# A hybrid transformer step on one core: prompt attention as one list of 64 blocks, sample pages fetched ahead of the sample delta net, other loads of the down projection

## Chip, core and metric

One core of a Trainium2 chip. The metric is the device time of one execution in microseconds; the kernel before took 1775.74 us (median of 3 runs, 1774.68 to 1777.79). One more execution was profiled; it took 1775.13 us, and all times of the trace are taken from it.

## The reference

One decoder layer runs over 1024 prompt tokens and 32 sample tokens (8 sequences of 4), with a width of 1024, and a last norm follows. Everything is fp32.

```python
def stick_breaking(q, k, v, q_pos, k_pos, sb_bias):
    z = einsum(q, k) * d ** -0.5 + sb_bias
    mask = k_pos[None, :] < q_pos[:, None]
    log_1m = where(mask, log_sigmoid(-z), 0.0)
    suffix = cumsum(log_1m, axis=3, reverse=True) - log_1m
    w = where(mask, exp(log_sigmoid(z) + suffix), 0.0)
    return einsum(w, v)
...
h = rmsnorm(x, norm_mix_w)
q_a, k_a, v_a, u, z, a, b, g_a, g_b = split(h @ w_in)
o_a = stick_breaking(...)          # prompt: causal; sample: past pages by page_table, then its own keys
o_b, ssm_new = gdn_branch(short_conv(u), z, a, b, ...)   # gated delta net
y_a = o_a @ w_pa
y_b = o_b @ w_pb
x = x + (sigmoid(g_a) * y_a + sigmoid(g_b) * y_b) @ w_o
x = x + square(relu(rmsnorm(x) @ w_up)) @ w_down
y = rmsnorm(x, norm_final_w)
```

The attention has 8 heads of 64, the delta net 4 heads of 128, the inner width of the MLP is 4096. New keys, values, convolution and delta-net states are outputs as well.

## The kernel before

Activations lie transposed: 8 tiles of 128 features by 1056 tokens, in four token chunks `CX` (256, 256, 256, 288). A dense product is made of three passes, high by high, low by high, high by low part of the split operands (`dense`, lines L137, L138, L139); ScalarE (ACT) rounds the high part and VectorE (DVE) subtracts for the low part when a weight arrives (`load_w`, L123 to L128). PSUM has four pairs of banks: `dtile`, `gtile`, `ttile` and others hand them out.

The stages, by their time in the profile: norm, projections and the prompt's delta net up to about 535 us; the sample delta net (its `drk`, `df` and the like are one-column powers that GpSimd, POOL, computes) to about 600; sample attention over gathered pages (L767 to L874) to 651; prompt attention (`weights`, `attn_head`, `attn_last`, from L881) from 681 on, with the gates' projections (L963 to L976, tiles `pd_g`), the transposes of the residual input (L977 to L988, `xrp`) and the second merge product `y_b` (L1018 to L1053, `pb`, whose operand `obh`, `obl` is read back from DRAM as `ofb`); the first merge product (`pa`) to about 1040; then the output projection, the up projection, and from 1416 the down projection, made of seven products a group of weight blocks (`pw`), with a last part of plain products (`pv`) and the last norm.

Nobody writes the order of the work out. A scheduler takes the program in its order, with the tiles' buffers, `high_priority` sections and `issue_after` marks, and orders each engine's instructions; each engine then runs its own in that order. Nearly all DMAs are issued by SyncE (SP), one after the other in its order: a DMA that waits for a buffer holds up all that stand behind it. The gathers of pages are issued by POOL.

A block of prompt attention is 128 queries of one head against the keys up to them (`weights(hh, i, ...)`, block `i` has 128 x (i + 1) keys). PE makes scores `sc` in two passes (L903, L904); ACT takes their sigmoid into `s` (L905); POOL masks the diagonal (L906) and makes `am` = 1 - s (L909); DVE scans the running product backwards (L913, `pr`) and multiplies (L914); PE transposes `s` by blocks of 128 (`tr`, L111) and ACT copies the result to `wt` (L921); PE multiplies by the values (`po`, L941, L956). Heads 0 to 5 store their output through `oT` in DRAM (`o_d`, read back as `ofa`); heads 6 and 7 run side by side and go straight to `oah3`, `oal3`. `qs`, `kh`, `kl` are loaded for each head and have two buffers.

The gates and residual transposes are in the program behind heads 0 to 5, so that the scheduler takes them when PE would wait; the `pb` products stand behind heads 6 and 7. In the sample attention, keys (`kg`, L819) and values (`vg`, L833) of two pages are gathered for each of 8 sequences, keys transposed to `kts` (L826), in two groups of four sequences.

For the down projection, group 0 loads four weight blocks in quarters (`load_q`, L1368 by its line in the trace, tiles `a11` to `a22`, named `a` in the profile), and for each of seven products four half blocks of the hidden layer (`load_h`, L1360, tile `hc`); `y` takes the residual `x1_d`. The last part loads its weights block by block, both column halves of each.

Of the kernel before, what the change touches and what calls it, by code (L numbers as in the profile page):

```python
# [38 lines left out]
def hybrid_step(ctx, tc, x_prompt, x_sample, cache_k, cache_v, page_table, state_conv, state_ssm,  # L39
# [523 lines left out]
    bk = pool("bk", stack=bctx, side="right")  # L563
    dctx = ExitStack()
# [160 lines left out]
    vk = pool("vk", stack=bctx, side="right")  # L725
# [44 lines left out]
    idx = bk.tile([P, 16], I32, name="idx")  # L770
    nc.scalar.dma_start(idx, page_table.rearrange("s g -> (s g)").unsqueeze(0).to_broadcast([P, 16]))
    rowi = bk.tile([P, 16], I32, name="rowi")
    G.iota(rowi, pattern=[[0, 16]], base=0, channel_multiplier=1)
    V.tensor_scalar(idx, idx, P, None, op0=ALU.mult)
    V.tensor_tensor(idx, idx, rowi, op=ALU.add)
    ckf = cache_k[0].rearrange("n t h d -> (n t) (h d)")
    cvf = cache_v[0].rearrange("n t h d -> (n t) (h d)")

# [32 lines left out]
    vgs = {}  # L811
    for g in range(2):
        psc = ttile(f"dsc{g}")
        kts = []
        for s4 in range(4):
            s = 4 * g + s4
            kg = bk.tile([P, 2, 512], F32, tag="kg", name=f"kg{s}", bufs=2)
            for pg in range(2):
                G.indirect_dma_start(kg[:, pg, :], None, ckf, bass.IndirectOffsetOnAxis(ap=idx[:, 2 * s + pg:2 * s + pg + 1], axis=0))  # L819
            kt = bk.tile([P, 4, 260], F32, tag="kts", name=f"kts{s}", bufs=6)  # L820
            for p2 in range(2):
                pt = (gtile if p2 else dtile)(f"dkt{s}_{p2}")
                for q in range(4):
                    p, pg = 2 * p2 + q // 2, q % 2
                    tr(pt[:, q * P:(q + 1) * P], kg[:, pg, p * P:(p + 1) * P])
                S_.activation(kt[:, 2 * p2:2 * p2 + 2, 0:256], pt.rearrange("p (a f) -> p a f", a=2), AF.Copy)  # L826
            V.tensor_copy(kt[:, :, 256:260], ksT[:, :, 4 * s:4 * s + 4])
            kts.append(kt)
        for s4 in range(4):
            s = 4 * g + s4  # L830
            vgs[s] = vk.tile([P, 2, 512], F32, tag="vg", name=f"vg{s}", bufs=4)
            for pg in range(2):
                G.indirect_dma_start(vgs[s][:, pg, :], None, cvf, bass.IndirectOffsetOnAxis(ap=idx[:, 2 * s + pg:2 * s + pg + 1], axis=0))  # L833
# [5 lines left out]
        ds_ = bk.tile([P, n], F32, tag="ds", name=f"ds{g}", bufs=2)  # L839
# [40 lines left out]
    ak = pool("ak", 2, stack=actx, side="right")  # L880

# [14 lines left out]
    def weights(hh, i, qs, kh, kl):  # L896
        n = P * (i + 1)
        qsl = slice(i * P, n)
        s = ak.tile([P, NP], F32, tag="s", name=f"s{hh}_{i}", bufs=6)
        for k0 in range(0, n, 512):  # L900
# [3 lines left out]
            PE.matmul(pt[:, :kn_], lhsT=qs[:, qsl], rhs=kl[:, k0:k0 + kn_], start=False, stop=True)  # L904
# [9 lines left out]
        V.tensor_tensor(s[:, :n - 1], s[:, :n - 1], pr[:, 1:n], op=ALU.mult)  # L914
        wt = ak.tile([P, NP], F32, tag="wt", name=f"wt{hh}_{i}", bufs=2)
# [7 lines left out]

    def load_v(p):
# [4 lines left out]
    def attn_head(hh, vn):  # L929
        p, a = hh // 2, hh % 2  # L930
        rs = slice(64 * a, 64 * a + 64)
        ops = attn_load(hh)
        oT = ak.tile([P, NC // 2, P], F32, tag="oT", name=f"oT{hh}")
        for m in range(NC // 2):
            wts = [weights(hh, 2 * m + r, *ops) for r in range(2)]
            po = gtile(f"po{hh}_{m}")
            for b in range(2 * m + 2):
                for r in range(2):
                    if b > 2 * m + r:
                        continue  # L940
                    PE.matmul(po[64 * r:64 * r + 64, 0:P], lhsT=vn[:, b, rs], rhs=wts[r][:, b * P:(b + 1) * P],  # L941
                              start=(b == 0), stop=(b == 2 * m + r))
            S_.activation(oT[:, m, :], po[:, 0:P], AF.Copy)
        for r in range(2):
            SY.dma_start(o_d[p, rs, 0:NP].rearrange("d (m r c) -> d r m c", r=2, c=P)[:, r], oT[64 * r:64 * r + 64])

    def attn_last(oh, ol):
        vn = load_v(3)
        ops = [attn_load(6), attn_load(7)]
        for i in range(NC):  # L950
            wts = [weights(6 + a, i, *ops[a]) for a in range(2)]
            po = gtile(f"po6_{i}")
            for b in range(i + 1):
                for a in range(2):
                    rs = slice(64 * a, 64 * a + 64)
                    PE.matmul(po[rs, 0:P], lhsT=vn[:, b, rs], rhs=wts[a][:, b * P:(b + 1) * P], start=(b == 0), stop=(b == i))  # L956
            cs_ = slice(i * P, (i + 1) * P)
            S_.activation(oh[:, cs_], po[:, 0:P], AF.Copy)
            V.tensor_tensor(ol[:, cs_], po[:, 0:P], oh[:, cs_].bitcast(F32), op=ALU.subtract)

    for p in range(3):
        vn = load_v(p)
        attn_head(2 * p, vn)  # L963
        attn_head(2 * p + 1, vn)


    for j in range(KT):
        for b, gd in ((0, gA_d), (1, gB_d)):
            gt = fk.tile([P, T], F32, tag="ft", name=f"gt{b}_{j}", bufs=NFT)

            def ev(c, o, n, pt, gt=gt):
                with tc.high_priority():
                    S_.activation(gt[:, o:o + n], pt[:, :n], AF.Sigmoid)

            proj([(3592 + b * D + j * P, f"g{b}_{j}", ev)], f=True)
            SY.dma_start(gd[j], gt)  # L976
    for t in range(9):  # L977
# [24 lines left out]
    attn_last(oah3, oal3)  # L1002
# [18 lines left out]
    for c in (3, 0, 1):  # L1021
        ob_tiles(c)
    with tc.high_priority():
        S_.activation(obh[0], ofb0, AF.Copy)
        V.tensor_tensor(obl[0], ofb0, obh[0].bitcast(F32), op=ALU.subtract)
    for c, (o, n) in enumerate(CX):
        if c == 0:
            continue
        for k in range(4):
            st = obp.tile([P, 288], F32, tag="of", name=f"ofb{c}{k}", bufs=3)  # L1030
            if c == 1 and k == 0:
                ob_tiles(2)
            mark = SY.dma_start(st[:, :n], o_d[4 + k, :, o:o + n])
            with tc.high_priority():
                S_.activation(obh[c][:, k], st[:, :n], AF.Copy)
                V.tensor_tensor(obl[c][:, k], st[:, :n], obh[c][:, k].bitcast(F32), op=ALU.subtract)
        if c == 1:
            with tc.issue_after(mark.ins):
                for j in range(2):
                    SY.dma_start(tbs[j], gB_d[j])  # L1040
    for jp in range(4):
        wb = load_w(wpbv[:, :, jp * 256:(jp + 1) * 256], f"pb{jp}")
        for jj in range(2):
            j = 2 * jp + jj
            tb = tbs[j]
            if jp:
                with tc.issue_after(mark.ins), tc.issue_after(wq[0].ins):
                    SY.dma_start(tb, gB_d[j])
            for c, (o, n) in enumerate(CX):
                pt = dtile(f"pb{j}_{c}", f=True)  # L1050
                dense4(pt, wb, jj, [obh[c][:, k] for k in range(4)], [obl[c][:, k] for k in range(4)], n)
                with tc.high_priority():
                    V.tensor_tensor(tb[:, o:o + n], pt[:, :n], tb[:, o:o + n], op=ALU.mult)  # L1053
    ofa = []
    for k in range(2):
        st = (zp if k == 0 else z2p).tile([P, T], F32, tag="zz", name=f"ofa{k}")
# [27 lines left out]
    for jp in range(4):  # L1084
        wa = load_w(wpav[:, :, jp * 256:(jp + 1) * 256], f"pa{jp}")
        for jj in range(2):
# [5 lines left out]
            for c, (o, n) in enumerate(CH):  # L1092
# [260 lines left out]

    def split2(tl):
# [181 lines left out]
```

## Time and profile before

| | |
|---|---|
| runs | 1775.74 us median, 1774.68 to 1777.79 |
| profiled execution | 1775.13 us, span 1773.2 us, granted clock 0.988 |
| sample attention, 600 to 660 us | PE busy 50.1 of 60 |
| prompt attention with gates, 680 to 760 | PE busy 78.1 of 80, DVE 48.1 |
| prompt attention with residual transposes, 760 to 840 | PE busy 72.4 of 80, DVE 61.6 |
| heads 6 and 7 with `pb`, 840 to 900 | PE busy 55.3 of 60, DVE 49.4 |
| up to the down projection, 1040 to 1380 | PE busy 336.7 of 340 |
| into the down projection, 1380 to 1420 | PE busy 34.8 of 40 |
| down projection, 1420 to 1690 | PE busy 269.9 of 270 |
| from 1763 to the end | PE busy 4.5 of 10 |

The busy time of PE is modelled: a matmul that stands alone shows 0.28 us, though in a row the next one starts 0.12 us later. So a stage with many lone matmuls shows more busy time than work.

### The profile page before, as it was taken

The page shows a single profiled execution, that of the slowest core. Times are in us where ns is not written, and L with a number is a line of the kernel's source. Part 1 is how long each engine was busy: PE and PEld are TensorE (multiplying, and loading weights), DVE is VectorE, ACT ScalarE, POOL GpSimd, SP SyncE. Part 2 cuts the span into 40 slices and gives each one's busy share as a digit, 9 for nine tenths or more (in the row PEclk, how much of TensorE's full clock was granted, in tenths as well). Part 3 has the DMA queues.
Part 4 walks back from the last instruction along what each step waited for, and adds up shares of the span by engine and source line. Part 5 has one row for each costly group of instructions (what it writes and reads, how often), then busy time and mean ns, then how long its engine had stood idle before and what let it go on. Part 6 is the DMA issues. An engine that isn't in the chain of part 4 may idle for free.

```text
span 1773.2 us, 34494 instructions
## 1 busy us (share of the span) xinstructions
PE 1710.3 (96%) x13884; PEld 1646.6 (93%) x13884; DVE 1156.5 (65%) x2312; ACT 785.3 (44%) x1563; POOL 205.0 (12%) x239
## 2 busy tenths in 40 slices
PE   7999999999999889999899999999999899999998
PEld 6999999999999668977789999999999899999998
DVE  6665777767234213677947577877777778788853
ACT  5553444343323223566523445555445555434454
POOL 1120111110001322356500000000000000000000
PEclk9999999999999889999999999999999999999999
DMA  5142232234335546578323544645444684432421
GB/s 175 43 119 77 56 115 78 90 104 145 113 106 153 181 133 160 143 186 231 125 96 121 163 145 134 171 140 149 148 141 134 216 303 146 156 112 94 135 84 75
DMA packets 233579, 239.22 MB, mean 135 GB/s; under 512 B 22754, under 2 KB 192067, under 8 KB 233420
## 3 DMA queue, kind: packets, MB, share of 16 engines
q1 hardware_dynamic: 229110, 228.40, 42.2%
q0 software_dynamic: 2560, 8.39, 1.5%
q8 instruction: 109, 1.79, 0.4%
q10 hardware_dynamic: 1750, 0.23, 0.1%
q14 instruction: 50, 0.41, 0.1%
HBM read 163.21 MB, written 73.77 MB: 134 GB/s over the span
## 4 chain that ended last, share of the span: by engine, by line
PE 70%; issue 12%; POOL 6%; DVE 6%; DMA 4%; ACT 1%; SPq 0%; POOLq 0%; DVEq 0%; ACTq 0%; another core or an unknown queue 0%
PE pu L139 6%; PE pu L137 6%; PE pu L138 6%; PE pw L138 5%; PE pw L137 5%; PE pw L139 5%; POOL am L909 3%; POOL s L906 2%; PE px L138 1%; PE px L139 1%; PE pv L137 1%; PE px L137 1%; PE pv L139 1%; PE pv L138 1%; PE pd_g L137 1%
## 5 line engine op out<-in xcount | busy, mean ns | idle before, releaser
L137 PE MATMUL pu<-Xh,uh 128*128 128x264 f32 x812 | 229.8, 283 | 1.0 <-ACT uh L1135 1.0
L139 PE MATMUL pu<-Xh,ul 128*128 128x264 f32 x812 | 230.1, 284 | 0.0
L138 PE MATMUL pu<-Xl,uh 128*128 128x264 f32 x812 | 229.7, 283 | 0.0
L137 PE MATMUL pw<-hc,w 128*128 128x264 f32 x728 | 206.7, 286 | 5.2 <-ACT w L1382 5.2
L138 PE MATMUL pw<-hc,w 128*128 128x264 f32 x728 | 207.0, 287 | 0.0
L139 PE MATMUL pw<-hc,w 128*128 128x264 f32 x728 | 201.7, 284 | 0.0
L137 PEld LDWEIGHTS pu<-Xh,uh 128*128 128x128 f32 x812 | 153.1, 189 | 1.2 <-ACT uh L1135 1.2
L138 PEld LDWEIGHTS pu<-Xl,uh 128*128 128x128 f32 x812 | 152.7, 188 | 0.0
L138 PE MATMUL pd_g<-xl,wh_g 128*128 128x256 f32 (+1 forms) x512 | 149.0, 291 | 3.2 <-issue 3.2
L139 PEld LDWEIGHTS pu<-Xh,ul 128*128 128x128 f32 x812 | 152.0, 188 | 0.0
L137 PE MATMUL pd_g<-xh,wh_g 128*128 128x256 f32 (+1 forms) x512 | 149.8, 293 | 1.4 <-issue 0.8
L139 PE MATMUL pd_g<-xh,wl_g 128*128 128x256 f32 (+1 forms) x512 | 149.9, 293 | 0.3 <-issue 0.3
L137 PEld LDWEIGHTS pw<-hc,w 128*128 128x128 f32 x728 | 137.8, 189 | 5.4 <-ACT w L1382 5.4
L138 PEld LDWEIGHTS pw<-hc,w 128*128 128x128 f32 x728 | 137.5, 189 | 0.0
L139 PEld LDWEIGHTS pw<-hc,w 128*128 128x128 f32 x728 | 135.4, 188 | 0.0
L913 DVE TENSOR_TENSOR_SCAN pr<-am 128x127 f32<-128x127 f32 (+7 forms) x64 | 89.8, 1403 | 43.0 <-POOL am L909 42.9
L138 PEld LDWEIGHTS pd_g<-xl,wh_g 128*128 128x128 f32 x512 | 97.6, 191 | 7.4 <-issue 7.1
L137 PEld LDWEIGHTS pd_g<-xh,wh_g 128*128 128x128 f32 x512 | 97.6, 191 | 6.2 <-issue 4.8
L139 PEld LDWEIGHTS pd_g<-xh,wl_g 128*128 128x128 f32 x512 | 97.5, 190 | 4.8 <-issue 4.6
L1382 ACT ACTIVATE w<-a 128x512 fp32r<-128x512 f32 x78 | 43.4, 623 | 94.3 <-PE pw L139 88.5
L114 POOL TENSOR_TENSOR fr<-fr,powc 128x3 f32<-128x3 f32 x4 | 3.4, 858 | 679.0 <-DVE fr L1493 643.2
L139 PE MATMUL px<-mh,wl_wo 128*128 128x264 f32 x256 | 72.7, 287 | 1.3 <-DVE wl_wo L1136 1.2
(581 smaller groups left out, 5198.7 us busy)
## 6 DMA issues: line engine op xcount, KB each, us to landing
hc_d<-t SPq DMA_DIRECT2D x26, 924.0 KB
hc<-hc_d SPq DMA_DIRECT2D x91, 264.0 KB
a<-in_w_down_dram SPq DMA_DIRECT2D x52, 256.0 KB
ws_g<-in_w_in_dram SPq DMA_DIRECT2D x16, 512.0 KB
ws_wo<-in_w_o_dram SPq DMA_DIRECT2D x32, 256.0 KB
ua<-in_w_up_dram SPq DMA_DIRECT2D x16, 512.0 KB
ub<-in_w_up_dram SPq DMA_DIRECT2D x16, 512.0 KB
gA_d<-gt SPq DMA_DIRECT2D x8, 528.0 KB
```

What stands on the lines that cost most here:

```text
L114: G.tensor_tensor(out, in_, powc[: out.shape[0], which:which + 1].to_broadcast([out.shape[0], n]), op=ALU.pow)
L137: PE.matmul(pt[:, :n], lhsT=wh[k], rhs=xh[k], start=(k == 0), stop=False)
L138: PE.matmul(pt[:, :n], lhsT=wh[k], rhs=xl[k], start=False, stop=False)
L139: PE.matmul(pt[:, :n], lhsT=wl[k], rhs=xh[k], start=False, stop=(k == nk - 1))
L906: G.affine_select(s[:, qsl], s[:, qsl], pattern=[[-1, P]], compare_op=ALU.is_gt, fill=0.0, base=0, channel_multiplier=1)
L909: G.tensor_scalar(am[:, :n], s[:, :n], -1.0, 1.0, op0=ALU.mult, op1=ALU.add)
L913: V.tensor_tensor_scan(pr[:, n - 1:0:-1], am_r, am_r, 1.0, op0=ALU.mult, op1=ALU.bypass)
L1382: S_.activation(tl[:, 0], src, AF.Copy)
```

## The change

**Sample pages.** Index, keys and values of sequences 0 to 3 move ahead of the sample delta net; the values' pool `vk` goes, `kts` has 4 buffers in place of 6. The keys and values of 4 to 7 stay in group 1 of the sample attention.

**Attention.** `weights` is cut in two: `scores` (up to the product on DVE) and `transposed` (transposes and copy). The 64 blocks become one list: heads 0 to 5, then 6 and 7 in turns with `i` descending. `pipeline` walks through it: scores of block x + 4, then transposes of block x (marked to stand behind those scores), then fillers, then the value products. Eleven of the 16 gates come before the list, five gates and nine residual steps fill blocks 0 to 33, and the 32 `pb` steps fill blocks 34 to 63. `s` keeps 6 buffers (LAG + 2). The residual step has one `xr` and one `xs` buffer, and stores in two halves. The operand of `pb` is read in four pieces instead of thirteen.

**Behind it.** The first merge product takes its token chunks in reverse.

**Down projection.** In group 0, the first four `hc` and the first weight quarter go to POOL's queue, the other loads are chained in the order of need, and `y` is loaded in halves between. In the last part, the first column halves of all weights and the hidden halves come first; the last square of the norm has a tile of its own, which PE adds in.

```diff
+    for s in range(4):
+        keys(s)
+        values(s)
     dctx = ExitStack()
     dk = pool("dk", stack=dctx, side="right")
...
-    vk = pool("vk", stack=bctx, side="right")
...
     for g in range(2):
         psc = ttile(f"dsc{g}")
+        if g:
+            for s in range(4, 8):
+                keys(s)
+        kts = [kts_[4 * g + s4] for s4 in range(4)]
...
+    blks = [(hh, i) for hh in range(6) for i in range(NC)] + [(6 + a, i) for i in range(NC - 1, -1, -1) for a in range(2)]
+    SPLIT = 34
...
+    def stage_b(x, fill):
+
+        ahead = state[min(x + LAG, NB - 1)][1]
+        with tc.issue_after(ahead.ins):
+            wts[blks[x]] = transposed(blks[x], state[x][0])
+        for f in fill:
+            f()
+        values_of(blks[x])
+
+    def pipeline(x0, x1, fill):
+
+        done = 0
+        for x in range(x0, x1):
+            stage_a(x + LAG)
+            upto = len(fill) * (x + 1 - x0) // (x1 - x0)
+            stage_b(x, fill[done:upto])
+            done = upto
...
+    def residual_step(t):
         n = P if t < 8 else NS
-        xn = fk.tile([P, D], F32, tag="ft", name=f"xr{t}", bufs=NFT)
+        xn = ak.tile([P, D], F32, tag="xr", name=f"xr{t}", bufs=1)
...
+    for j, b in gjobs[:11]:
+        for f in gate_steps(j, b):
+            f()
+    for x in range(LAG):
+        stage_a(x)
...
+    pipeline(0, SPLIT, fills)
...
-    attn_last(oah3, oal3)
...
+    steps = [lambda j=j, c=c, f=(x == 0): pb_step(j, c, f) for j in range(KT) for x, c in enumerate(range(4))]
+    pipeline(SPLIT, NB - 2, steps[:-6])
+    pipeline(NB - 2, NB, steps[-6:])
...
-            for c, (o, n) in enumerate(CH):
+            for c, (o, n) in reversed(list(enumerate(CH))):
...
+                        if i == 0:
+                            load_part(q, f, nm, G)
+                        else:
+                            queued(lambda: load_part(q, f, nm))
+            for n, f in enumerate(fs):
+                ld = lambda: load_h(hc_d[f - NPL, i], f"hc{f}_{i}", G if gi == 0 and i == 0 else SY)
+                hs[n] = queued(ld) if gi == 0 and i else ld()
...
+    for c in range(2):
+        for i, f in enumerate(fl):
             cs_ = slice(c * HD2, (c + 1) * HD2)
...
+                PE.matmul(pf[:n, i:i + 1], lhsT=sa[:, t * P:t * P + n], rhs=ones[:, 0:1], start=True, stop=False)
+                PE.matmul(pf[:n, i:i + 1], lhsT=sl[:, t * P:t * P + n], rhs=ones[:, 0:1], start=False, stop=True)
```

The rows below are the engines' instructions in the order of the built programs; a name ends with a number that tells buffers of one name apart.

POOL, between the masks of the delta net and the first mask of the prompt attention, before: `kg` and `vg` are gathers of keys and values, x2 the two pages of a sequence; `drk` and `df` belong to the sample delta net.

```order
L576 AFFINE_SELECT ms_4286<-ms_4286 128x256
L819 DMA kg_6126<-in_cache_k_dram,idx 128x512 x2
L819 DMA kg_6143<-in_cache_k_dram,idx 128x512 x2
L114 TENSOR_TENSOR drk<-drk_4352,powc 128x1
L114 TENSOR_TENSOR df<-df,powc 128x1
L819 DMA kg_6160<-in_cache_k_dram,idx 128x512 x2
L819 DMA kg_6177<-in_cache_k_dram,idx 128x512 x2
L833 DMA vg_6194<-in_cache_v_dram,idx 128x512 x2
L833 DMA vg_6197<-in_cache_v_dram,idx 128x512 x2
L833 DMA vg_6200<-in_cache_v_dram,idx 128x512 x2
L833 DMA vg_6203<-in_cache_v_dram,idx 128x512 x2
```

The same place now:

```order
L624 AFFINE_SELECT ms_4368<-ms_4368 128x256
L594 DMA kg_4283<-in_cache_k_dram,idx 128x512 x2
L607 DMA vg_4299<-in_cache_v_dram,idx 128x512 x2
L594 DMA kg_4302<-in_cache_k_dram,idx 128x512 x2
L607 DMA vg_4318<-in_cache_v_dram,idx 128x512 x2
L607 DMA vg_4337<-in_cache_v_dram,idx 128x512 x2
L607 DMA vg_4356<-in_cache_v_dram,idx 128x512 x2
L114 TENSOR_TENSOR drk<-drk_4434,powc 128x1
L594 DMA kg_4321<-in_cache_k_dram,idx 128x512 x2
L594 DMA kg_4340<-in_cache_k_dram,idx 128x512 x2
L594 DMA kg_6261<-in_cache_k_dram,idx 128x512 x2
```

Twelve gathers stand ahead of `drk` instead of four; five key pairs follow, then `df`, then one key pair and four value pairs, ten gathers in a row.

PE, at the end of head 3 and the start of head 4, before: `sc_2_0` is the score of block 2 from key 0 on, `wt_7_4` transposes of block 7 from key block 4 on, `po_3` the value products of blocks 6 and 7.

```order
L111 MATMUL wt_6_0_7265<-ident,s_6_7249 128x128 x2
L111 MATMUL wt_6_4_7271<-ident,s_6_7249 128x128 x3
L903 MATMUL sc_2_0_7372<-kh_7326,qs_7325 128x384
L904 MATMUL sc_2_0_7372<-kl_7327,qs_7325 128x384
L903 MATMUL sc_3_0_7389<-kh_7326,qs_7325 128x512
L904 MATMUL sc_3_0_7389<-kl_7327,qs_7325 128x512
L941 MATMUL po_3_7304<-wt_6_7264,vn_6865 64x128
L111 MATMUL wt_7_0_7292<-ident,s_7_7276 128x128 x4
L111 MATMUL wt_7_4_7298<-ident,s_7_7276 128x128 x4
L903 MATMUL sc_4_0_7416<-kh_7326,qs_7325 128x512
L904 MATMUL sc_4_0_7416<-kl_7327,qs_7325 128x512
```

PE now, in the middle of head 3, with gate products `pd_g`:

```order
L137 MATMUL pd_g_7_3_9070<-xh_167,wh_g_7_8780 128x288
L138 MATMUL pd_g_7_3_9070<-xl_168,wh_g_7_8780 128x288
L932 MATMUL sc_0_0_9050<-kh_9041,qs_9040 128x128
L933 MATMUL sc_0_0_9050<-kl_9042,qs_9040 128x128
L111 MATMUL wt_4_0_9061<-ident,s_4_8871 128x128 x4
L139 MATMUL pd_g_7_3_9070<-xh_167,wl_g_7_8781 128x288
L137 MATMUL pd_g_7_3_9070<-xh_167,wh_g_7_8780 128x288
L138 MATMUL pd_g_7_3_9070<-xl_168,wh_g_7_8780 128x288
L980 MATMUL po_1_9029<-wt_3_9022,vn_8266 64x128
L980 MATMUL po_1_9029<-wt_2_8983,vn_8266 64x128
```

In heads 3 to 5 PE had only `sc`, `wt`, `po` and `xrp`; now gate products stand between them up to block 33, and `pb` from there on.

SP, where `pb` begins, now (with what each waits for; a wait for DMAHW is for an earlier DMA in the same one of eight lanes): `ofb` is an operand of `pb`, `tb` a gate read back, `kh`, `kl` and `qs` are the operands of head 6 (9848 to 9850) and head 7 (9896 to 9898).

```order
L919 DMA kh_9849<-kh_d 64x1024 [waits DMAHW6_49]
L1119 DMA ofb_9417<-o_d 128x4x256 [waits DMAHW7_49]
L920 DMA kl_9850<-kl_d 64x1024 [waits DMAHW0_49]
L1148 DMA ofa_10723<-o_d 128x1056 [waits DMAHW1_49,DVE_49]
L1119 DMA ofb_9423<-o_d 128x4x288 [waits DMAHW2_49,DVE_49]
L1135 DMA tb_9394<-gB_d 128x1056 [waits DMAHW3_49]
L1135 DMA tb_9395<-gB_d 128x1056 [waits DMAHW4_49]
L1135 DMA tb_9396<-gB_d 128x1056 [waits DMAHW5_49]
L1135 DMA tb_9397<-gB_d 128x1056 [waits DMAHW6_49]
L985 DMA o_d<-oT_9367 64x4x128 [waits DMAHW7_49,Activation_49]
L1148 DMA ofa_10725<-o_d 128x1056 [waits DMAHW2_49,DMAHW1_49,DVE_49]
L919 DMA kh_9897<-kh_d 64x1024 [waits PE_49]
```

The loads of head 7 stand behind the gates read back and the store of head 4 (`oT_9367`); before, the gates read back stood behind them.

SP at the start of the down projection, before, with the first weight quarters `a` behind the twelfth `hc` load:

```order
L1360 DMA hc_2_17064<-hc_d 128x528
L1308 DMA hc_d<-t_16571 128x7x264
L1360 DMA hc_2_17068<-hc_d 128x528
L1360 DMA hc_2_17072<-hc_d 128x528
L1368 DMA a_3_16720<-in_w_down_dram 128x512
L1368 DMA a_3_16722<-in_w_down_dram 128x512
```

POOL now holds the first eight of these loads:

```order
L1453 DMA hc_0_16722<-hc_d 128x528
L1453 DMA hc_0_16726<-hc_d 128x528
L1453 DMA hc_0_16730<-hc_d 128x528
L1453 DMA hc_0_16734<-hc_d 128x528
L1461 DMA a_3_16702<-in_w_down_dram 128x512
L1461 DMA a_4_16707<-in_w_down_dram 128x512
L1461 DMA a_5_16712<-in_w_down_dram 128x512
L1461 DMA a_6_16717<-in_w_down_dram 128x512
```

They no longer stand behind the twelve `hc` loads of SP, and the second quarters follow on SP.

More of the change, by code (lines that the diff above doesn't have):

```diff
@@ L810, in hybrid_step @@
     osT = bk.tile([P, 4, NS], F32, name="osT")
-    vgs = {}
     for g in range(2):
         psc = ttile(f"dsc{g}")
-        kts = []
+        if g:
+            for s in range(4, 8):
+                keys(s)
+        kts = [kts_[4 * g + s4] for s4 in range(4)]
         for s4 in range(4):
             s = 4 * g + s4
[L817 to L833, printed above, removed]
+            V.tensor_copy(kts[s4][:, :, 256:260], ksT[:, :, 4 * s:4 * s + 4])
+            if g:
+                values(s)
         for p in range(4):
@@ L947, in attn_last @@
[L947 to L976, printed above, removed]
@@ L1019, in ob_tiles @@
         obl[c] = obp.tile([P, 4, CX[c][1]], F32R, name=f"obl{c}")
-    for c in (3, 0, 1):
+    for c in range(len(CX)):
         ob_tiles(c)
-    with tc.high_priority():
-        S_.activation(obh[0], ofb0, AF.Copy)
-        V.tensor_tensor(obl[0], ofb0, obh[0].bitcast(F32), op=ALU.subtract)
     for c, (o, n) in enumerate(CX):
         if c == 0:
[L1028 to L1053, printed above, removed]
+            st = ofb0
+        else:
+            if c == 1:
+                st = z2p.tile([P, 4, 288], F32, tag="zz", name="ofb1")[:, :, 0:256]
+            elif c == 2:
+                st = obp.tile([P, 4, 256], F32, name="ofb2")
+            else:
+                st = z2p.tile([P, 4, 288], F32, tag="zz", name="ofb3")
+            mark = SY.dma_start(st, o_d[4:8, :, o:o + n].rearrange("k p c -> p k c"))
@@ new lines, in hybrid_step, with pb_step @@
+        with tc.high_priority():
+            S_.activation(obh[c], st, AF.Copy)
+            V.tensor_tensor(obl[c], st, obh[c].bitcast(F32), op=ALU.subtract)
+        if c == 2:
+            for j in range(2):
+                SY.dma_start(tbs[j], gB_d[j])
+    wbs = {}
+    def pb_step(j, c, first):
+        jp, jj = j // 2, j % 2
+        if jp not in wbs:
+            wbs[jp] = load_w(wpbv[:, :, jp * 256:(jp + 1) * 256], f"pb{jp}")
+        tb = tbs[j]
+        if jp and first:
+            with tc.issue_after(mark.ins), tc.issue_after(wq[0].ins):
+                SY.dma_start(tb, gB_d[j])
+        o, n = CX[c]
+        pt = dtile(f"pb{j}_{c}", f=True)
+        dense4(pt, wbs[jp], jj, [obh[c][:, k] for k in range(4)], [obl[c][:, k] for k in range(4)], n)
+        with tc.high_priority():
+            V.tensor_tensor(tb[:, o:o + n], pt[:, :n], tb[:, o:o + n], op=ALU.mult)
```

233 lines of the change are left out of this document (168 added, 65 removed).

## Prediction

> **What bounds the kernel now.** I read the engine shares first, then the windows by stage, the timeline for the pace of one matmul, and the waits of the stages that fall short. Columns of the windows: the stretch, its length, busy us (instructions) of PE, PEld, DVE, ACT, POOL, the granted clock, the DMA share, GB/s.
>
> ```profile
> PE 1710.3 (96%) x13884; PEld 1646.6 (93%) x13884; DVE 1156.5 (65%) x2312; ACT 785.3 (44%) x1563; POOL 205.0 (12%) x239
> ```
>
> ```profile
> 680.00:760.00 80.00, 78.14 (x633) 70.42 (x632) 48.07 (x47) 39.10 (x90) 27.23 (x44) 1.00 0.54 139
> 760.00:840.00 80.00, 72.37 (x564) 58.49 (x563) 61.61 (x58) 52.76 (x118) 49.19 (x54) 0.96 0.86 227
> 840.00:900.00 60.00, 55.28 (x444) 46.25 (x444) 49.42 (x66) 30.63 (x70) 26.02 (x30) 1.00 0.33 112
> 900.00:940.00 40.00, 37.31 (x283) 35.39 (x280) 19.94 (x35) 9.43 (x13) 0.00 (x0) 1.00 0.37 120
> 1420.00:1690.00 270.00, 269.93 (x2214) 269.71 (x2213) 216.76 (x406) 121.13 (x219) 0.00 (x0) 1.00 0.47 160
> ```
>
> TensorE bounds the kernel: the change can only win what it loses in a few places. In the long dense stage it loses nothing (2214 matmuls in 270 us, 0.122 each). The busy column hides losses, since a matmul that trickles still shows 0.28 us, so I count work by pace, start to start, from a stretch without idle:
>
> ```profile
> 713.94 0.34 PE L903 MATMUL sc<-kh,qs 128*128 128x384 f32 x1
> 714.11 1.03 PE L111 MATMUL wt<-ident,s 128*128 128x128 f32 x8
> 714.90 0.42 PE L904 MATMUL sc<-kl,qs 128*128 128x384 f32 x1
> 715.16 0.39 PE L903 MATMUL sc<-kh,qs 128*128 128x512 f32 x1
> 715.39 0.40 PE L904 MATMUL sc<-kl,qs 128*128 128x512 f32 x1
> 715.63 0.29 PE L137 MATMUL pd_g<-xh,wh_g 128*128 128x288 f32 x1
> ...
> 716.42 0.28 PE L137 MATMUL pd_g<-xh,wh_g 128*128 128x256 f32 x1
> ...
> 717.82 1.96 PE L941 MATMUL po<-wt,vn 128*64 128x128 f32 x28
> 719.71 0.55 PE L111 MATMUL wt<-ident,s 128*128 128x128 f32 x3
> ```
>
> A transpose costs 0.79/8 = 0.099 us, a 512-wide score 0.235 (0.45 ns a column), a 288-wide product 0.79/6 = 0.132, a value product 1.89/28 = 0.0675. Attention has 64 blocks: 8 x 2 x 4608 score columns (33 us), 288 transposes (28.5), 576 value products (39), 101 us, or 1.6 a block. Beside it stand in 680 to 940 us the fillers:
>
> ```profile
> L139 PE MATMUL pd_g<-xh,wl_g 128*128 128x256 f32 (+1 forms) x115 | 33.3, 290 | 0.0
> L139 PE MATMUL pb<-obh,wl_pb 128*128 128x256 f32 (+1 forms) x128 | 37.1, 290 | 0.0
> L111 PE MATMUL xrp<-ident,xr 128*128 128x128 f32 (+1 forms) x72 | 9.2, 268 | 0.8 <-DMA xr<-in_x_prompt_dram 0.8
> L913 DVE TENSOR_TENSOR_SCAN pr<-am 128x127 f32<-128x127 f32 (+7 forms) x64 | 89.8, 1403 | 43.0 <-POOL am L909 42.9
> L914 DVE TENSOR_TENSOR s<-s,pr 128x127 f32<-128x127 f32 (+7 forms) x64 | 53.0, 832 | 4.0
> ```
>
> (columns: line, engine, operation, tiles, shapes and count | busy us, mean ns of one | idle before and its releaser). Gates 3 x 115 x 0.122 = 42 us, merge products 3 x 128 x 0.122 = 47, residual transposes 7, and the first 62 products of the next stage 10 (0.17 each, as the 384-wide score): 207 to 209 us of work in 260, so **about 51 us are lost here**. The stretch that mixes gates in best, 700 to 760, holds (rows of one pass; scores and gates have two and three):
>
> ```profile
> L139 PE MATMUL pd_g<-xh,wl_g 128*128 128x256 f32 x61 | 17.5, 286 | 0.0
> L941 PE MATMUL po<-wt,vn 128*64 128x128 f32 x144 | 13.1, 280 | 0.0
> L111 PE MATMUL wt<-ident,s 128*128 128x128 f32 x77 | 11.2, 279 | 0.4 <-DVE s L914 0.4
> L903 PE MATMUL sc<-kh,qs 128*128 128x512 f32 x12 | 5.4, 448 | 0.0
> L913 DVE TENSOR_TENSOR_SCAN pr<-am 128x767 f32<-128x767 f32 (+7 forms) x17 | 23.7, 1392 | 18.9 <-POOL am L909 18.9
> ```
>
> 21.5 us of gates 256 wide, 6.3 of gates 288 wide, 9.7 of value products, 7.6 of transposes, 9 of scores (25 matmuls 512 wide and 26 narrower): 54 of 60, 5.8 lost over 17 blocks. By the same count 24 us are lost from 760 to 840, 12 from 840 to 900, 4.5 from 680 to 700, 4.3 from 900 to 940. The reason is VectorE: scan and product take 142.8/64 = 2.23 us a block against PE's 1.6. Heads 3 to 5 have 7 us of residual transposes beside them, and PE waits.
>
> **Attention.** The list of 64 blocks keeps the work and spreads the fillers. Gates left for the attention: five (480 products, 58 us) over 34 blocks with the residual steps (7): 54 + 65 = 119 us PE against 34 x 2.23 = 76 DVE. The merge products (47) go over the last 30, longer blocks: 47 + 47 = 94 us and some 5 of the next stage, against 68 us of scans and products on VectorE and what these rows hold:
>
> ```profile
> L1053 DVE TENSOR_TENSOR tb<-pb,tb 128x256 f32<-128x256 f32 (+1 forms) x32 | 13.4, 426 | 18.2 <-PE pb L139 17.1 <-DMA tb<-gB_d 1.0
> L128 DVE TENSOR_TENSOR wl_pb<-ws_pb,wh_pb 128x1024 fp32r<-128x1024 f32 x4 | 4.9, 1223 | 0.5 <-ACT wh_pb L127 0.5
> ```
>
> 13.4 and 4.9, and 9 for the splits of the attention's outputs (my estimate, some eight tiles of that size): 95. PE leads in both halves, if closely in the second. The lag of four blocks is 4 x 3.5 = 14 us (60 us over 17 blocks), and of a block's chain (score copy, mask, `am`, scan, product) the two costliest steps are 2.2. So what stays is what 700 to 760 shows, 5.8 us over the 17 blocks scanned there, 0.34 a block: 22 us; a start as before (680 to 700: 4.5 lost, 3 beyond that rate); the end as before, 4; and I put 4 for the point where the merge products begin (below). 51 - 33 = **18 us gained**; ends 8 (DVE bounds the last 30 blocks with the losses of 840 to 900, 0.2 of the time) and 32 (change-overs cost half, nothing else stays). A residual step now has one `xr` and one `xs` buffer, so each waits for the store of the one before; 2 to 4 blocks lie between, 7 us or more, and I cost it at nothing. The reversed order in the next stage, too: it takes first what the descending blocks finish first.
>
> **Sample pages.** Each gather holds POOL 0.95 + 0.30 us. Two runs of twelve stand here, and PE, DVE and ACT crawl from some 7.6 us after a run's first gather to 6 us after its last:
>
> ```profile
> 599.37 1.02 POOL L819 DMA_INDIRECT kg<-in_cache_k_dram,idx  x1 [16.30 <-PE dkt L111]
> ...
> 613.23 0.95 POOL L833 DMA_INDIRECT vg<-in_cache_v_dram,idx  x1 [0.30 <-issue]
> ...
> 630.65 0.94 POOL L819 DMA_INDIRECT kg<-in_cache_k_dram,idx  x1 [9.00 <-PE dkt L111]
> ...
> 644.44 0.95 POOL L833 DMA_INDIRECT vg<-in_cache_v_dram,idx  x1 [0.30 <-issue]
> ```
>
> ```profile
> 535.00:555.00 20.00, 19.48 (x163) 19.21 (x161) 11.79 (x43) 12.38 (x23) 4.66 (x5) 1.00 0.82 246
> 607.00:621.00 14.00, 9.20 (x39) 6.54 (x38) 0.00 (x0) 2.94 (x6) 8.80 (x10) 0.63 0.74 238
> 638.00:652.00 14.00, 8.94 (x41) 5.75 (x43) 1.18 (x3) 2.45 (x5) 5.70 (x6) 0.63 0.48 144
> ```
>
> 39 and 41 matmuls at 0.12 are 4.8 us of each 14: 9.2 lost twice, 18.4. The four gathers near 540 cost nothing. The change does not break the runs: POOL's order has twelve in a row at about 540 (keys and values of four sequences), then pairs, then ten (the last keys and all later values). The first moves its 9.2 us to about 548; ten crawl for 12.5 + 6 - 7.6 = 11 us instead of 13.4, 7.5 lost. Gain 1.7, say **2**. Ends: 18 if the crawl came from something else at 600, and -7: `drk`, a power on POOL of the sample delta net, now stands behind twelve gathers, some 9 us late, and its chain waits while PE has gate products; with no cover that is all lost.
>
> **Down projection, start.** PE stands still between 1411 and 1416 for the first weight quarter, behind 12 loads of `hc` in SP's queue:
>
> ```profile
> 1407.69 4.67 SPq L1368 DMA_DIRECT2D a<-in_w_down_dram  x5
> ```
>
> ```profile
> 1408.00:1412.00 4.00, 3.05 (x26) 2.85 (x24) 4.00 (x10) 1.95 (x4) 0.00 (x0) 1.00 1.07 370
> 1412.00:1416.00 4.00, 0.00 (x0) 0.00 (x0) 2.37 (x5) 3.17 (x6) 0.00 (x0) 1.00 1.05 371
> 1416.00:1420.00 4.00, 3.73 (x18) 3.73 (x19) 4.00 (x9) 0.85 (x2) 0.00 (x0) 0.57 1.00 373
> 1690.00:1695.00 5.00, 3.71 (x29) 3.28 (x27) 4.61 (x9) 3.41 (x6) 0.00 (x0) 1.00 0.49 185
> ```
>
> 44 matmuls in 12 us are 5.3 us of work: 6.7 lost, clock at 0.57 included. Now POOL issues the four `hc` and four first quarters, 2.1 MB, 5.6 us at 370 GB/s, released by a product that the order puts some 95 matmuls, 11.6 us, before the up projection's end. I take **4**; ends 0, and 6.7. A loss is bounded by an eight-long run that crawls as above for 8 us: -4. The Trainium skill, DMA: Bandwidth & Descriptors, section Issuing engines are not separate DMA queues, speaks against this part: all issuers share the 16 engines, and a second one "will only save the time on the sequencer". By it this term would be 0 and the sum 1754; the share of 1.0 agrees that the engines are full, but the row of SP shows an order, not a rate, that kept the quarter back.
>
> **Last part.** 29 products in 5 us from 1690 are 3.5: 1.5 lost to weights that come late; the first column halves now come first: **1** (0 to 1.5). The tail's squares skip one VectorE addition and add nine one-column products: nothing, +-0.5.
>
> **Sum.** 18 + 2 + 4 + 1 = 25 us. The profiled execution took 1775.1 (span 1773.2), 0.6 below the median of the runs, 1775.7: 1775.1 - 25 = **1750**.
>
> **Rivals.** (1) SP's queue where the merge products begin; slower. Between head 4's last score and head 7's first, 29 us of PE work (26 by pace, 9 blocks of change-over), SP must issue in order head 6 (1.5 MB), two pieces of the merge operand and `ofa` (1.6), four gates read back (2.1), head 4's store, `ofa` and head 7 (2.3): 7.8 MB. The stage 760 to 840 moved 227 GB/s at a share of 0.86, 264 when full: 29.5 us, just enough, hence my 4 us. All PE work stands in order behind those operands. At 160 GB/s it takes 49 us, a stall of 20: 1766. From 141 GB/s down (55 us) the 26 us cancel every gain: at 120, 65 us, about **1782**. Against it: no busy stage here was so slow. (2) VectorE bounds the last 30 blocks, as 840 to 900 (49.4 of 60 busy, 12 lost): gain 8, and no gain at the pages: **1765**. For it: 95 against 99. (3) The crawl goes with the place and the change-overs shrink: 32 + 12 + 5: **1730**. (4) Page run and `drk` cost 7, the eight-run 4, the switch 15 more: gains cancel, about **1775**. That the change isn't made is excluded by the order of the built program.
>
> **Chances.** Forecast (1738 to 1762) 0.58; rival 3 0.10; rival 2 with half of rival 1 (1762 to 1772) 0.14; rival 4 0.07; rival 1 slower 0.11. A measurement of this kernel tells some 0.2% (3.5 us) from no change: faster 0.82, within 0.07, slower 0.11. The range reaches from the unknown costs' good ends to rival 2's far side: 1732 to 1771.
>
> **What would show it.** Right: 760 to 840 at over 640 matmuls in 80 us, no scan-bound stretch; a crawl with clock near 0.6 at about 550 and one of ten gathers later; no empty window at the start of down. Wrong: PE waiting for `kh`, `obl` or `tb` around the first merge products (rival 1), `wt` waiting for `s` on DVE in the last heads (rival 2), `drk`'s readers idle with PE idle too.

## The result, and the profile after

The changed kernel took 1753.82 us (median of 4 runs, 1751.82 to 1755.30) against 1776.53 before; the ratio is 0.9859, with a 95% interval of 0.9842 to 0.9876. Forecast were 1750, and 25 us gained; measured are 22.7. The profiled execution took 1754.63 us, 20.5 less than the profiled one of before. So the total came out close to the forecast. Its terms did not, as the experiments show.

The windows of the changed kernel, with the same columns as before, at the stages that the prediction spoke of:

```profile
541.00:555.00 14.00, 13.39 (x113) 13.11 (x112) 7.38 (x22) 11.23 (x21) 11.26 (x10) 1.00 0.88 269
555.00:569.00 14.00, 9.69 (x86) 6.79 (x86) 1.96 (x5) 1.39 (x3) 6.52 (x8) 0.66 0.60 194
618.00:632.00 14.00, 13.73 (x129) 9.94 (x127) 2.74 (x6) 2.81 (x5) 8.48 (x8) 1.00 0.63 196
660.00:680.00 20.00, 17.51 (x119) 15.49 (x120) 12.01 (x13) 10.21 (x23) 10.22 (x16) 0.91 0.77 206
680.00:740.00 60.00, 60.00 (x502) 53.32 (x499) 40.66 (x37) 35.59 (x79) 25.89 (x34) 1.00 0.71 187
740.00:800.00 60.00, 59.65 (x481) 52.16 (x481) 32.93 (x35) 31.93 (x71) 19.27 (x30) 1.00 0.60 155
800.00:820.00 20.00, 16.95 (x138) 13.32 (x139) 18.62 (x19) 12.58 (x27) 14.37 (x14) 1.00 1.05 322
820.00:900.00 80.00, 80.00 (x673) 71.47 (x671) 58.96 (x74) 34.94 (x71) 25.69 (x37) 1.00 0.29 85
740.00:820.00 80.00, 76.60 (x618) 65.49 (x618) 51.55 (x53) 44.51 (x96) 33.64 (x44) 1.00 0.71 197
760.00:840.00 80.00, 76.80 (x593) 64.99 (x592) 59.00 (x57) 43.26 (x91) 37.97 (x41) 1.00 0.67 186
```

PE is full from 680 to 800 and from 820 to 900, with 8.0 to 8.4 matmuls a us, where before the stretches from 760 to 900 held 7.1 to 7.4. Two holes are left in the attention, at its start (660 to 680) and where the merge products begin (800 to 820). The second lies in the stretch for which I had named a sign, over 640 matmuls from 760 to 840: there are 593 (564 before), so this sign did not come. One crawl is left beside the gathers, at 555 to 569 with the clock at 0.66; beside the later gathers (618 to 632) there is none. What PE waited for from 640 to 675, and then from 795 to 822 (the wait, us in total, times, the longest):

```profile
PE xrp L111 <- DMA xr<-in_x_prompt_dram: 2.3, 1, 2.3
PE sc L933 <- DMA kl<-kl_d: 0.7, 1, 0.7
...
PE pb L138 <- DVE obl L1122: 2.1, 2, 1.7
PE pb L137 <- ACT wt L954: 0.5, 1, 0.5
PE pb L137 <- ACT obh L1121: 0.4, 1, 0.4
```

Where the down projection starts, the windows (and one of the last part), then ACT's timeline (start, us, engine, line, operation, count, idle before it):

```profile
1388.00:1392.00 4.00, 2.19 (x19) 1.99 (x17) 0.96 (x3) 2.56 (x5) 0.00 (x0) 1.00 1.04 364
1392.00:1396.00 4.00, 3.41 (x16) 3.41 (x17) 3.88 (x8) 3.49 (x8) 0.00 (x0) 0.57 0.83 309
...
1422.00:1430.00 8.00, 6.99 (x55) 6.56 (x55) 8.00 (x14) 7.36 (x15) 0.00 (x0) 1.00 0.53 183
...
1669.00:1674.00 5.00, 4.60 (x36) 4.19 (x35) 4.69 (x9) 4.95 (x11) 0.00 (x0) 1.00 0.49 184
```

```profile
1381.98 2.24 ACT L1448 ACTIVATE hc<-hc 128x528 fp32r<-128x528 f32 x4
1389.24 0.65 ACT L1390 ACTIVATE t<-t 128x528 f32<-128x528 f32 x1 [5.03 <-DVE t L1386]
...
1391.37 0.64 ACT L1391 ACTIVATE t<-t 128x528 f32<-128x528 f32 x1
1391.92 1.13 ACT L1475 ACTIVATE w<-a 128x512 fp32r<-128x512 f32 x2
```

The empty window is gone, and the loads come in time: ACT split the four `hc` by 1384. But the first weight quarter's split stands in ACT's order behind the last squares of the up projection, and so behind PE's last up product. The wait for a load has become a wait for ACT's order, 2.8 us from the last `pu` to the first `pw` where it was 5.6; and in 1422 to 1430, with DVE full, 55 products stand where 66 would fit (1.3 us).

### The profile page after: what moved, and what is told of

Read it like the earlier page. It is cut to its first block, busy times and chain, and to the rows that moved or that the text cites. A ratio compares the mean times of both kernels' runs of the same rounds, so it can differ in the third digit from the quotient of the medians.

```text
span 1752.9 us, 34523 instructions
## 1 busy us (share of the span) xinstructions
PE 1704.8 (97%) x13902; PEld 1645.2 (94%) x13902; DVE 1148.9 (66%) x2299; ACT 783.2 (45%) x1554; POOL 206.6 (12%) x247
## 3 DMA queue, kind: packets, MB, share of 16 engines
q10 hardware_dynamic: 1750, 0.23, 0.1%
## 4 chain that ended last, share of the span: by engine, by line
PE 74%; issue 8%; DMA 6%; DVE 6%; POOL 3%; ACT 1%; SPq 1%; POOLq 0%; DVEq 0%; ACTq 0%
PE pu L139 6%; PE pu L137 6%; PE pu L138 6%; PE pw L139 4%; PE pw L138 4%; PE pw L137 4%; PE pd_g L137 2%; POOL am L938 2%; PE pd_g L139 2%; PE pd_g L138 2%; POOL s L935 1%; PE px L138 1%; PE px L137 1%; PE px L139 1%; PE pv L137 1%
## 5 line engine op out<-in xcount | busy, mean ns | idle before, releaser
L138 PE MATMUL px<-ml,wh_wo 128*128 128x264 f32 x256 | 72.6, 285 | 0.0
```

Of the source, the lines that this page charges most:

```text
L138: PE.matmul(pt[:, :n], lhsT=wh[k], rhs=xl[k], start=False, stop=False)
```

## Experiments

The kernels of the table ran on three chips, here A, B and C, each beside the kernel before, which took 1778.9, 1763.6 and 1780.8 us there; so sizes are read as ratios to it, or between kernels of one chip.

| kernel | chip | us | ratio to before (95%) |
|---|---|---|---|
| pages as before (`gath_back`) | A | 1772.96 | 0.9964 (0.9950 to 0.9977) |
| attention as before (`attn_back`) | A | 1763.14 | 0.9899 (0.9875 to 0.9923) |
| down's loads as before (`down_back`) | A | 1756.01 | 0.9863 (0.9840 to 0.9886) |
| last part as before (`last_back`) | A | 1753.04 | 0.9853 (0.9828 to 0.9878) |
| gathers broken up (`paced`) | B | 1745.70 | 0.9908 (0.9883 to 0.9933) |
| all gates ahead (`gates16`) | B | 1765.13 | 1.0013 (0.9999 to 1.0028) |
| pages as before, 14 gates ahead (`gath_back_g14`) | B | 1752.84 | 0.9946 (0.9924 to 0.9968) |
| lag of one block (`lag1`) | B | 1752.52 | 0.9944 (0.9926 to 0.9962) |
| changed kernel (`after_again`) | C | 1754.22 | 0.9850 (0.9827 to 0.9872) |
| gathers broken up (`paced_again`) | C | 1756.69 | 0.9867 (0.9846 to 0.9889) |
| broken up, two small moves (`paced_late`) | C | 1752.80 | 0.9844 (0.9818 to 0.9869) |
| broken up, attention as before (`paced_attn_back`) | C | 1764.84 | 0.9913 (0.9885 to 0.9941) |

**One part undone at a time.** Each of the four leaves out the diff's hunks of one part.

```diff
-    for s in range(4):
-        keys(s)
-        values(s)
```

> The sample pages fetched as before, all else as changed. Forecast's sizes: the two crawls cost 18.4 us in place of some 16, so 2 us above the changed kernel, about 1756. Reading of the changed trace (one crawl at 555 to 568 us and none behind the later gathers): 5 to 9 us above, 1759 to 1763. Two stretches of 14 us with about 40 matmuls come back near 607 and 638 us.

```diff
-    pipeline(0, SPLIT, fills)
+    for p in range(3):
+        vn = load_v(p)
+        attn_head(2 * p, vn)
+        attn_head(2 * p + 1, vn)
```

> Prompt attention, gates, residual transposes and both merge products as before, all else as changed. Forecast's size: 18 us above the changed kernel, about 1772. Reading of the changed trace (35 us lost between 650 and 920 against 51 between 680 and 940): 15 above, about 1769. If the gain came from the sample pages and the down projection, it stays within 5 us of the changed kernel.

```diff
-                            load_part(q, f, nm, G)
+        qs2 = [load_q(f) for f in fs]
```

> Loads of the down projection's groups as before, all else as changed. Forecast's size: 4 us above the changed kernel, about 1758. Reading of the changed trace (the gap shrank from 5.6 to 2.8 us, but 13 matmuls or 1.5 us are lost at the third product): 1 above, about 1755. By the rule that a second issuer saves only the time of issuing: 0.

```diff
-    hid[1] = [load_h(half(h_d[f], 1), f"hp{f}_1") for f in fl]
+    hid = [[load_h(half(h_d[f], h), f"hp{f}_{h}") for f in fl] for h in range(2)]
```

> Last part and last norm as before, all else as changed. Forecast's size: 1 us above the changed kernel, about 1755. Rival: nothing or 1 us below, since in the changed trace the end behind the last product takes 11.6 us against 10.2 before.

Beside 0.9859 for the whole change (0.9850 on chip C), the pages are worth 0.0105 of 1779, 18.7 us, the attention 0.0040, 7 us, and the last two parts 0 to 1, not told apart from nothing. The intervals of the attention's and the last two ratios are +-4 us, so that a worth of 4 us for the down projection's loads is not excluded either. Taken the other way round it is the same: without the attention, 18 us of gain are left, without the pages 6. The forecast's 2 and 18 for pages and attention are both missed, and so are the 5 to 9 and the 15 that I read from the changed trace. Windows of `gath_back`, then its waits from 640 to 700:

```profile
607.00:621.00 14.00, 8.53 (x50) 6.52 (x48) 0.00 (x0) 2.73 (x6) 8.78 (x10) 0.84 0.77 269
638.00:652.00 14.00, 8.63 (x45) 5.23 (x44) 1.00 (x3) 2.11 (x5) 6.96 (x8) 0.71 0.60 168
...
670.00:680.00 10.00, 0.00 (x0) 0.00 (x0) 0.00 (x0) 0.00 (x0) 0.00 (x0) 0.56 0.97 222
680.00:700.00 20.00, 17.31 (x98) 15.06 (x99) 10.43 (x12) 8.58 (x20) 8.36 (x14) 0.79 0.72 181
```

```profile
PE sc L922 <- DMA kh<-kh_d: 11.7, 1, 11.7
PE dsc L852 <- ACT kts L842: 2.9, 1, 2.9
```

Both crawls are back. And a hole that neither kernel has: from 670 to 680 no engine computes, only loads run. The attention's first loads cannot start before the sample attention has given its memory back (SP issues the first `kh` at 670.78 here, at 646.99 in the changed kernel), and the eleven gates put ahead of the list are used up by then; the kernel before had sixteen in the pool to draw on. So one part of the change needs the other: eleven gates are enough only because the sample attention now ends some 23 us earlier (the first score stands at 658 in place of 681).

**Is that hole the gates'?** Fourteen gates ahead of the list, two in it.

```diff
-    for j, b in gjobs[:11]:
+    for j, b in gjobs[:14]:
```

> Sample pages fetched as before, the attention as one list, but fourteen gates ahead of it instead of eleven. If the list alone gains nothing because its eleven gates run out while PE waits for the sample pages and then for the first head's loads (11.7 us in one wait, some 20 lost from 660 to 700), three more gates, 35 us of work, fill that hole: 11 to 16 us faster than with eleven, 1757 to 1762. If the hole is made by the loads themselves, it stays: about 1773.

```profile
660.00:670.00 10.00, 10.00 (x85) 10.00 (x84) 1.23 (x1) 2.08 (x5) 0.00 (x0) 1.00 1.04 267
670.00:680.00 10.00, 9.69 (x80) 9.48 (x79) 3.07 (x5) 2.64 (x6) 1.47 (x4) 1.00 1.05 260
...
740.00:820.00 80.00, 71.40 (x539) 54.37 (x539) 70.74 (x60) 55.98 (x121) 58.43 (x56) 0.94 0.81 233
```

The hole is filled, as the theory wanted: 85 and 80 matmuls where there were none. The three gates are then missing from 740 to 820 (539 matmuls in 80 us, DVE at 71, where the changed kernel's 740 to 820 holds 618). As this ran on chip B and `gath_back` on A, the forecast difference of 11 to 16 us cannot be taken from their times; against each chip's kernel before they gain 10.8 and 6.

**Fillers or lag?**

```diff
-    for j, b in gjobs[:11]:
+    for j, b in gjobs[:16]:
```

> The changed kernel with all sixteen gates ahead of the attention list, so that blocks 0 to 33 have only the nine residual steps as filler (61 us of PE work against 76 of scans and products). If the gain of the list comes from the fillers: 15 to 22 us slower than the changed kernel, 1768 to 1775, PE waiting for the product on DVE there. If it comes from the lag of four blocks: within 4 us, up to 1758.

```diff
-    LAG = 4
+    LAG = 1
```

> The changed kernel with a lag of one block and three buffers of s. A block's chain through ACT, POOL and DVE is at least 4.4 us in the mean and a block of PE work with its fillers 3.5, so if the lag is needed PE waits 1 us or more a block: 30 to 60 us slower, 1785 to 1815. If the fillers alone carry it: within 5 us of the changed kernel.

On chip B the nearest kernel to the changed one is `paced` (1745.7; on chip C it stands 2.5 us above the changed kernel). Against it, all gates ahead cost 19 us, as expected. A window of `gates16`, and PE's waits from 650 to 940:

```profile
740.00:820.00 80.00, 73.14 (x564) 55.60 (x563) 75.07 (x64) 54.87 (x121) 64.02 (x63) 0.96 0.81 212
```

```profile
PE xrp L111 <- DMA xr<-in_x_prompt_dram: 4.6, 2, 3.2
PE xrp L111 <- ACT xs L1051: 2.8, 2, 1.8
PE sc L932 <- issue: 2.6, 1, 2.6
PE wt L111 <- DVE s L943: 2.1, 1, 2.1
PE wt L111 <- ACT xs L1051: 1.8, 1, 1.8
```

DVE is busy 75 of 80 us and PE gets 564 matmuls in. But only 2.1 us of the named waits are for the product on DVE, which I had expected; 9.2 are for the residual steps' single buffers `xr` and `xs`, between which no gate stands any more. So the 19 us are what the gates are worth as fillers for the scans and for the residual steps together.

A lag of one block, with three buffers of `s`, costs 7. My 30 to 60 was far off: PE waits for the product on DVE 0.6 us in all in this trace. That the fillers between a block's scores and its transposes hide its chain is my explanation and was not tested. The other theory's 5 is nearly met. So the fillers carry most of the list's worth, and the lag some 7 us, both measured against `paced`.

**What makes the engines crawl?** The first twelve gathers were meant to be broken up, six and then pairs behind waits:

```diff
-    for s in range(4):
-        keys(s)
-        values(s)
+    keys(0)
+    keys(1)
+    values(0)
+    keys(2)
+    with tc.issue_after(kgs[2].ins):
+        values(1)
+    keys(3)
+    with tc.issue_after(kgs[3].ins):
+        values(2)
+        values(3)
```

> The changed kernel with its first twelve gathers broken up: six, then pairs that wait for transposes, by putting later keys ahead of the values on POOL. If a long unbroken run of gathers makes the engines crawl, the crawl at 555 to 568 us (some 8 us lost) goes: 1746 to 1749, at the most two matmul windows of 5 us below 35 instructions left. If the crawl comes from the bytes or from the place, it stays and the time is that of the changed kernel, 1752 to 1756.

1745.7 us looked like a hit. But POOL's timeline shows that the run was not short (the first and the last of 14 gathers, 0.3 us apart in between), and the first window shows 186 matmuls beside it, most of them short ones of the delta net (211 where no gather runs). The second window is the same stretch of `lag1`, which has the changed kernel's twelve gathers in a row, on the same chip:

```profile
551.26 1.21 POOL L594 DMA_INDIRECT kg<-in_cache_k_dram,idx  x1 [1.67 <-PE dkt L111]
...
568.56 0.95 POOL L594 DMA_INDIRECT kg<-in_cache_k_dram,idx  x1 [0.30 <-issue]
```

```profile
555.00:569.00 14.00, 11.80 (x186) 10.02 (x185) 4.40 (x8) 4.51 (x8) 10.66 (x11) 1.00 0.76 232
```

```profile
555.00:569.00 14.00, 13.42 (x183) 12.39 (x185) 4.72 (x16) 7.07 (x15) 10.53 (x11) 1.00 0.86 260
```

So the order without the edit hardly crawls on this chip either. `drk` ran late there too (561.55 in `lag1`), so its delay alone does not make the changed kernel's crawl. And the kernel before was 15 us faster on this chip than on the others. `gath_back_g14`, with the gathers in the order of before, has 116 matmuls in each of the two stretches where that order crawled on chip A (50 and 45):

```profile
607.00:621.00 14.00, 13.60 (x116) 11.48 (x115) 1.05 (x3) 3.67 (x8) 10.61 (x12) 1.00 0.91 309
638.00:652.00 14.00, 14.00 (x116) 11.19 (x111) 3.84 (x7) 3.02 (x7) 1.25 (x2) 1.00 0.44 131
```

So the missing crawl was the chip's and not the edit's. On chip C the control therefore stands beside the test.

`after_again` is the changed kernel as it is, `paced_again` the kernel of the last edit.

> The changed kernel itself, as a control on the chip of the next three. Two chips gave the kernel before 1779 and 1764 us. If this is the crawl behind the gathers, which one chip shows and the other hardly, the changed kernel is at 1752 to 1755 where the kernel before is near 1777 (ratio near 0.986), and at 1745 to 1750 where it is near 1764 (ratio 0.990 to 0.992), since it has one crawl and the kernel before two.

> The changed kernel with its first gathers broken up, a second time, beside its control. If breaking up the run removes the crawl: 5 to 9 us faster than the control where the control shows a stretch of 10 us with fewer than 75 matmuls near 560, 2 or less where it shows none. If only the chip made the first result: equal to the control within 2 us.

The changed kernel took 1754.2, as expected of a chip with the crawl. The edited one took 1756.7, and crawls all the same (a window of `paced_again`, then POOL's timeline: the first and the last of ten gathers, 0.3 us apart in between, and the next one):

```profile
555.00:569.00 14.00, 9.95 (x96) 6.71 (x95) 2.18 (x9) 3.96 (x7) 9.14 (x11) 0.83 0.72 220
```

```profile
552.17 1.64 POOL L594 DMA_INDIRECT kg<-in_cache_k_dram,idx  x1 [1.67 <-PE dkt L111]
...
564.17 0.95 POOL L607 DMA_INDIRECT vg<-in_cache_v_dram,idx  x1 [0.30 <-issue]
567.24 0.95 POOL L594 DMA_INDIRECT kg<-in_cache_k_dram,idx  x1 [2.11 <-remote]
```

So the edit did not shorten the run enough to test my theory: six gathers, then ten without a pause. What stands is that the chip decides first. The same program (`paced`, `paced_again`) has 186 matmuls in this stretch on chip B and 96 on chip C, and runs of twelve and more do little harm on B; the length of a run alone does not make the crawl. Whether shorter runs would be free of it on chips A and C, no run tested: a run of ten crawled there, and the later eight, which have 129 matmuls from 618 to 632 in the changed kernel, have 106 in `paced_again`.

**The two holes left in the attention, and the list's worth.**

Both rest on the broken gathers. The first moves the merge products by two blocks and the residual steps by one:

```diff
-            if t % 2 == 0 and t // 2 < 9:
-                fills.append(lambda t=t // 2: residual_step(t))
+        if x % 2 == 0 and 2 <= x < 20:
+            fills.append(rsteps[x // 2 - 1])
...
-    pipeline(SPLIT, NB - 2, steps[:-6])
+    pipeline(SPLIT, SPLIT + 2, [])
+    pipeline(SPLIT + 2, NB - 2, steps[:-6])
```

> The same with two small moves in the attention: the first residual step one gate step later, and the merge products from block 36 on instead of 34. The changed trace loses 6 us near 800 to 820, where the first merge product waits for its operand's low part on DVE, and 2.3 waiting for the first residual load. If those waits are on the path: 3 to 5 us faster than the kernel with broken gathers; if DVE has to do the same work anyway: within 1 us.

The second takes the attention's hunks out, as `attn_back` does:

```diff
-    pipeline(0, SPLIT, fills)
+    attn_last(oah3, oal3)
```

> Broken gathers with the attention, gates, residual steps and merge products as before: the worth of the list without the crawl in between. By the count of the two traces (51 us lost between 680 and 940 before, 35 between 650 and 920 changed) 12 to 16 us slower than the kernel with broken gathers; by the medians of the earlier pair 7 to 9; by the forecast 18.

The two moves gain 3.9 us over `paced_again`, within the 3 to 5 expected, but the intervals of the two ratios overlap, and the result is only 1.4 us below the changed kernel's on this chip: no version here beats it beyond doubt. Part of the 3.9 us repairs a loss that the changed kernel does not have: from 800 to 820 `paced_again` holds 109 matmuls, `paced_late` 138, as the changed kernel does.

With the attention as before the time is 8.1 us higher, which agrees with the 7 of chip A. The forecast's 18 is missed, and so are the 12 to 16 by counting lost time in two traces. But that count had an error. At the prediction's own prices the changed kernel's 650 to 920 hold 518 gate products (63 us), 384 merge products (47), attention (101), residual transposes (7) and 67 products of the next stage (11): 229 us of work in 270, so 41 are lost, not 35. The same count gives 44 for `paced_again` (650 to 920) and 52 for `paced_attn_back` (660 to 940), 8 apart as the times are. A window behind these 8 us, `paced_attn_back` first, then `paced_again`:

```profile
780.00:880.00 100.00, 87.97 (x677) 68.25 (x676) 83.15 (x90) 62.23 (x144) 55.80 (x60) 0.97 0.70 199
```

```profile
780.00:880.00 100.00, 94.48 (x757) 82.25 (x754) 74.61 (x76) 49.99 (x101) 36.31 (x46) 0.98 0.50 139
```

## Why the prediction was right, and where not

**The sum was right by two errors against each other, which is luck.** 25 us were forecast, as 18 + 2 + 4 + 1; the runs give about 7 to 8 for the attention, 18 for the pages, and 0 to 1 for the rest together.

**Pages: forecast 2, measured 18.** The step that failed is "The change does not break the runs", by which both crawls stay almost whole: it took the run of gathers for the cause and left out the chip. Two crawls of 9.2 us each were rightly read off; but the prediction's ten later gathers, which came as two and, after 4.5 us, eight, crawl not at all (129 matmuls in 14 us), and the first run, though it grew to sixteen with `drk` between, has one crawl, at 555 to 569 in place of 548. `drk` ran at 557.69 in place of about 547, and that delay shows in no wait of PE that I could name. In the single traces the first score of `gath_back` stands 22.5 us behind that of the changed kernel (680.6 and 658.1). Some 10 of them are the crawl that went: at 0.12 a matmul `gath_back` loses 8.0 and 8.6 in its two, and the changed kernel some 7 in its one (about 100 short matmuls fewer than on chip B, at 14/211 us). Another 10 are the empty window from 670 to 680, which no sum of mine had: with the pages undone, the list's eleven gates run out, so these 10 us belong to the two parts together. With the attention as before there is no such hole, and yet 18 us of gain are left by the ratios, but only 7 by the spans of the two single traces (1773.2 before, 1766.0 on chip A; the kernel before scattered from 1772.7 to 1787.9 on the chips A and C). So what the pages bring without the list is not settled. Rival 3 held that "the crawl goes with the place"; for one of the two crawls it did.

**Attention: forecast 18, measured 7 to 8,** just under the lower end of 8. The mechanism was right: gates in place of idle time (19 us when taken away), PE full from 680 to 800 and from 820 on. The size was not. What stays lost was forecast at 33 us; the same count gives 41 in the changed trace, so that 10 are gained by it. Most of the 8 us between them is the rate of 0.34 us a block, read off the best stretch: the full stretches (680 to 800, 820 to 900: PE is busy there, but slower than the prices) lose 24 us over 51 blocks, 0.47 each, 6 to 7 more than forecast. The start (650 to 680) loses 8.0, where the rate and my 3 make 5.4. The point where the merge products begin loses 6.9 (138 matmuls from 800 to 820), where I put 2 by rate and 4 for the point. Rival 1's stall did not come, but the signs that I gave for it and for a scan-bound stretch showed in a small way there: PE waited for `obl`, 2.1 us, since the splits of the merge operand stood on DVE between scans, and DVE had 18.6 of 20 us to do. The loads ran at 322 GB/s; ACT waited 2.1 us for a piece of the merge operand, and 5.3 in `paced_again`, where PE waited 3.5 us for `obh` in turn. The step from the 10 by count to the 7 to 8 of the medians is within their interval.

**Down's start: forecast 4, measured 0 to 2,** with an interval of +-4 us. The gap shrank by 2.8 us, then ACT's order took the place of the load, and 1.3 us went at the third product. The rule of the Trainium skill, DMA: Bandwidth & Descriptors, section Issuing engines are not separate DMA queues, gave this term 0; the total does not contradict it (0.9863 with the old loads, 0.9859 with the new), while the trace shows the order of issue at work, and a new one behind it.

**Last part: forecast 1, measured nothing** (1753.0 with it undone). 1669 to 1674 holds 36 products where 1690 to 1695 held 29, but the end behind the last product takes 11.6 us (1741.3 to the span's end) in place of 10.2 (1763.0 to 1773.2).

So rivals 1 and 2 did not decide the time: no load stalled PE for long, and PE is full in the last 30 blocks from 820 on.

## What to carry to other kernels

A total that agrees says little about its terms: undo each part alone before you believe the split. Before you take work out of a pool of fillers, look at who draws on the pool earlier, and how long that stage lasts; here the list of blocks needed the sample stage to end 23 us sooner. When you count lost time, count both traces at the same prices: one slip here made 10 us into 16. And when a test changes the time in the expected direction, run the control on the same chip, and read in the trace whether the edit did what it was to do: one chip made an edit that left ten gathers in a row look like a gain of 8 us.

## What the runs showed of the hardware

Beside gathers, PE can drop to a third or so of its pace (39 to 50 matmuls in 14 us, at 0.12 each time for 117) with a granted clock of 0.63 to 0.84 over the stretch, while DVE and ACT do little, without a wait that the trace names. It depends on the chip. The same program shows it on one (96 matmuls from 555 to 569, `paced_again`) and hardly on another (186, `paced`), and the order of gathers of before has 50 and 45 matmuls in its two stretches on chip A and 116 and 116 on chip B, there with three more gates ahead of the list. The kernel before is 15 to 17 us faster on chip B. Fourteen gathers without a pause did little harm there; ten in a row crawled on chip C. The cause is open: no run here changed the bytes of a gather, or where its pages lie, or had only short runs on a chip that crawls.
